# A hybrid attention and convolution layer: chain blocks placed behind scores, output projection before token sums, a first up-projection by column part

## The chip, the cores and the metric

The kernel runs on one core of a Trainium2 chip. The metric is the time of one execution on the device in microseconds (us), as the median of several. A core has a matrix engine (TensorE, PE in the profile, with PEld for its weight loads), a vector engine (VectorE, DVE), a scalar engine (ScalarE, ACT), a general engine (GpSimd, POOL) and an engine that only issues transfers (SyncE, SP); each works through its own instructions in order and waits for the others by semaphores.

## The reference

One layer of a diffusion backbone works on 1024 latent tokens and 256 context tokens of width 1024, all in float32:

```python
h = _rmsnorm(x, norm1_g) * (1.0 + sc1) + sh1
proj = h @ w_in
a = attend(q, k, v)                      # 8 heads of 64
hyo = _hyena(hy, k_f, filt_bias)         # 512 channels, two long convolutions by FFT
merged = concat([_rmsnorm(a, g_a), _rmsnorm(hyo, g_h)])
x = x + g1 * (merged @ w_out)
h2 = _rmsnorm(x, norm2_g) * (1.0 + sc2) + sh2
u = _dwconv3(h2 @ w_up, ffn_conv_w, ffn_conv_b)
gate, up = jnp.split(u, 2, axis=-1)
x = x + g2 * ((jax.nn.silu(gate) * up) @ w_down)
```

Context tokens attend among themselves; a latent token attends to a window of 8 by 16 latent tokens with a learned bias by relative position, and to 256 cached context keys, in one softmax. The norm of the attention group is taken over its 512 channels for each token. After the layer stands a last norm.

## The kernel before, in words

The kernel is written against a planner: the program traces instructions in some order, that order is their priority, and the planner simulates the engines and gives each of them, whenever it falls free in the simulation, the ready instruction of the highest priority. `tc.high_priority(offset=n)` lets a block count as if it had been traced n instructions earlier (later, if n is negative). `tc.issue_after(ins)` sets what the block traces on the engine of `ins` behind `ins` in that engine's order. Memory is given out by pools on two stacks, a left and a right one; with `reuse_waits="tile"` a new tile waits only for the old tiles whose bytes it takes.

Precise products are made of three fast ones: operands are split in a high part (ACT) and a low part (DVE or POOL), and `mm3` (lines 116 to 118) multiplies high by high, high by low and low by high.

The stages around the change, in order of time:

- **Input projection and chains.** The long convolutions are five chains (`chain(j)`, four blocks of 128 latent channels and one for the context), each of eight phases: for each of two convolutions a forward transform on PE (line 805, with `dftf`) with twiddles on ACT and DVE (817 to 819), sums and the product with the filter spectrum on DVE (826 to 847, the spectrum K loaded by SP at 840), the sums back with twiddles (852 to 864), and a backward transform on PE (877) with gating on DVE (882 to 890). Two lanes run them: chains 0, 2, 4 and chains 1, 3. `phases(n)` traces the next n phases in a fixed order of lanes (`turn2`). Sixteen are traced with a lead of 2000 instructions in the stage of the projection, the sixteenth being the first phase of chain 2. The rest is traced between the parts of the attention. The early ones have three PSUM banks for the transforms (`cA`), the later ones a single bank.
- **Attention** (`attend(p_)`, four pairs of heads). For each half b of a pair: score products on PE (`smm`, line 1068), bias and maximum on DVE (1089), exponentials on ACT (1102, 1103), then transposes of the weights on PE (1112), their copies to `pt` on ACT and DVE (1020, 1022), weighted values (1030), the reciprocal of the sums by way of PE (1040, 1045), and the result into `at4` (1159; context 1139). A pair's bias tables `tb` come by 48 small transfers that POOL issues (967), and wait for the last reader of the pair before. The context attention is traced last in pairs 0 to 2 and first in pair 3. A pair yields three times: after the scores of b = 0, after its values, and after the scores of b = 1.
- **Weights of the output projection.** Eight blocks of rows, k = 0 to 7, are loaded by SP (1205) and split by `wo_split` (ACT 1197, DVE 1198). Rows of k below 4 meet attention channels, the others convolution channels. The pool stands on the right stack, on the bytes of the chains. The raw rows `wor` have two buffers by turns, so the load of block k waits for the split of block k - 2; block 7 goes in two halves through a smaller one.
- **Token sums** (`token_scales`). The squares of the attention output, summed over channels for each token, give its scale `rsa` and the inverse `ria` by which the convolution half is brought to the same scale. `asq` holds the squares of pairs 0 to 2 summed, `sq` those of pair 3. For each block of 128 tokens PE multiplies a column of ones by the tile (line 1227), both tiles into the same sum; then DVE, POOL (a power, 1231), DVE, PE (a reversal of order, 1234) and DVE.
- **Output projection**, ten blocks of 128 tokens in the order 8, 9, 0, 4, 1, 2, 3, 5, 6, 7 (8 and 9 are the context). `att_split` (1291, 1292) splits a block of `at4` into `ar`; `omm(n, 0)` makes its half of the product with k = 0 to 3. `hyena_split` loads the convolution output y (1304), scales it (which needs `ria`), transposes it (1312) and splits it into `mr`; `omm(n, 1)` adds that half. Each half is 24 matmuls of 512 columns; three blocks can be under way (six banks). `post` adds the residue (it needs `rsa` and the gate rows g1), norms the row (1357, 1358), transposes it (1366) and writes it to hA (blocks 8, 9, 0, 4) or hB (the others).
- **Up-projection.** A Strassen-like scheme with seven products for each of 22 column blocks f, in the order 0, 1, 4, 5, 2, 6, 3. The left factors are sums `S` of quarters of the weight, split into `ws` tiles (121, 122); the right ones are sums of quarters of hA (256 columns, part s = 0) and of hB (384 columns, part s = 1), split into `Ta[p]` and `Tb[p]` (1263, 1264). `Ta[0..2]` and `Tb[0..1]` are split inside the loop of the output projection, the others behind it. `up(f, ...)` runs product after product, each for both parts; `cp` copies a sum out of its bank into `pc` (part 0) and a piece of `acc` (part 1). The tiles of pool `ffn` (`S`, `pc`, every third `ws`) take the bytes of hA and hB; those of pool `wsx` hold the gate rows g1 first.

Of the kernel before, what the change touches and what calls it, by code (L numbers as in the profile page):

```python
# [11 lines left out]
F32 = mybir.dt.float32  # L12
# [7 lines left out]
P = 128  # L20
D = 1024
# [65 lines left out]
def _build(nc, tc, top, V, A, G, T, Q, I, O, dbg, upto):  # L87
# [677 lines left out]
    with tc.high_priority(offset=2000):  # L765
        Q.dma_start(out=dftf.rearrange("p a b -> p (a b)"), in_=I["t_dft"].flatten().rearrange("(p x) -> p x", p=P))
        Q.dma_start(out=idft.rearrange("p a b c -> p (a b c)"), in_=I["t_idft"].flatten().rearrange("(p x) -> p x", p=P))

    S4B, TB = 3, 1
    CHP = 2000  # L770

    def chain(j):
# [22 lines left out]
        for o in range(2):  # L795
# [3 lines left out]
            for h in range(2):  # L799
                hs = slice(h * P, (h + 1) * P)  # L800
                for rp in range(2):
                    pa = bk("cA")
                    xs = slice(rp * 256, (rp + 1) * 256)
                    for i in range(2):
                        T.matmul(pa[:, i * 256:(i + 1) * 256], dftf[:, i, hs], uv[:, i, xs], start=True, stop=True)
                    pv = pa.rearrange("p (i r c) -> p i r c", i=2, r=2)
                    if not lat:
                        A.copy(Gv[:, h, :, 2 * rp:2 * rp + 2], pv)
                        continue
                    for ri in range(2):  # L810
                        r = 2 * rp + ri
                        if r == 0:
                            A.copy(Gv[:, h, :, 0], pv[:, :, 0])
                            continue
                        c, s, ns = tw_chain(h, r)
                        t = cp.tile([P, 2, P], F32, tag=f"t{b_}", name="t", bufs=TB)
                        A.activation(t[:, 0], pv[:, 1, ri], AF.Copy, scale=ns)
                        A.activation(t[:, 1], pv[:, 0, ri], AF.Copy, scale=s)
                        V.scalar_tensor_tensor(Gv[:, h, :, r], pv[:, :, ri], c, t, op0=ALU.mult, op1=ALU.add)
# [88 lines left out]
                next(lanes[turn2.pop(0)], None)  # L908

    with tc.high_priority(offset=CHP):  # L910
        phases(16)
    cbk.close()
    cbk = Banks("bkd", "right", "tile", cA=(1, 1))
    for _ in ada:
# [137 lines left out]
    def attend(p_):  # L1052
# [12 lines left out]

        def smm(outs, qc, kc):
            for h in range(2):
                T.matmul(outs[h], q[hs[h], qc], kc(hs[h]), start=True, stop=True, tile_position=(DH * h, 0),
                         skip_group_check=True)

        def scores(cb, l, l2, j):

# [71 lines left out]
        for b in range(2):  # L1144
            l, l2 = stat("l", 8), stat("l2", 8)
            for j in range(2):
                scores(2 * b + j, l, l2, j)
            yield
            V.tensor_add(l, l, l2)
            av = bk("av")  # L1150
            for j in range(2):
                cb = 2 * b + j
                for kt in range(2):
                    ps = turn(lambda h, i: Pc[cb][:, h, i, kt * P:(kt + 1) * P])
                    av_mm(av, 256 * j, vs[:, 10 + kt], ps, kt == 0)
                for vt, ps in local(cb):
                    av_mm(av, 256 * j, vt, ps, False)
            bs = recips(l, 8)
            V.tensor_mul(dst[:, 2 * b:2 * b + 2], av.rearrange("p (b r c) -> p b r c", b=2, r=16),
                         bs.rearrange("p (b r c) -> p b r c", b=2, r=16))  # L1160
            if b == 0:
                yield
# [6 lines left out]

    for p_ in range(4):  # L1170
        for n, _ in enumerate(attend(p_)):
            phases(2 - n % 2)
        phases(2)
    ces.close()
    cbk.close()
# [15 lines left out]
    sh2 = wo_.tile([P, 2, KC], F32, name="sh2")  # L1191
    V.tensor_copy(sh2.rearrange("p s (c j) -> p s c j", j=2), mods[:, 3].rearrange("p j (c s) -> p s c j", s=2))
    wo = []

    def wo_split(hi, lo, k, cs, w):
        g = grg[:, k:k + 1]
# [3 lines left out]
    for k in range(KC):  # L1200

        parts = [(slice(0, D), ("wh7", "wl7")[k % 2])] if k < 7 else [(slice(c, c + 512), "ot") for c in (0, 512)]
        for cs, tag in parts:
            w = wo_.tile([P, cs.stop - cs.start], F32, tag=tag, name="wor", bufs=1)
            Q.dma_start(out=w, in_=wsrc[:, k, cs])
            if cs.start == 0:
                hi, lo = [wfirst[i // 3][:, i % 3] for i in (2 * k, 2 * k + 1)] if k < 3 else \
                    [wo_.tile([P, D], F32R, tag=f"w{x}{k}", name=f"w{x}{k}", bufs=1) for x in "hl"]
            wo_split(hi, lo, k, cs, w)
        wo.append((hi, lo))  # L1210

    def tokens(t, i):
# [4 lines left out]

    def token_scales():

        sq = tp.tile([P, LT], F32, tag="q1", name="sq", bufs=1)  # L1220
        for cs in (slice(LL, LT), slice(0, LL)):
            A.activation(sq[:, cs], at4[:, 3, cs], AF.Square)
        ps = bk("X")
        for a, b in ((8, 10), (0, 8)):
            for i in range(a, b):
                for t in (asq, sq):
                    T.matmul(ps[:, 2 * i:2 * i + 2], tokens(t, i), ones2, start=t is asq, stop=t is sq,
                             skip_group_check=True)
            m, r = ria[:, a:b], rsa[:, a:b]
            V.tensor_scalar(m, ps[:, 2 * a:2 * b:2], 1.0 / 512, EPS, op0=ALU.mult, op1=ALU.add)  # L1230
            G.tensor_tensor(r, m, mhalf.to_broadcast([P, b - a]), op=ALU.pow)
            V.tensor_mul(m, m, r)
            pr = bk("X")
            T.matmul(pr[:, 0:b - a], jrev, m, start=True, stop=True)
            u = 4 if a == 0 else 1
            V.tensor_copy(m[:, u:], pr[:, u:b - a])

    token_scales()
    es.close()
    abk.close()  # L1240

# [155 lines left out]
    def second_sums(t):  # L1397
        cs = slice(t * P, (t + 1) * P)
        if t == 0:
            ts = acp.tile([P, 3, 4, NS[1]], F32, tag="acc", name="tsb", bufs=1)  # L1400
            b.update({4: ts[:, 0], 5: ts[:, 1], 3: ts[:, 2]})
        V.tensor_sub(b[4][..., cs], b12[..., cs], b11[..., cs])
        V.tensor_sub(b[5][..., cs], b22[..., cs], b[4][..., cs])
# [60 lines left out]

    def wstile():
        ring["ws"] += 1
        if ring["ws"] % 3:
            return wsx.tile([P, 2, 512], F32R, tag="ws", name="ws", bufs=2)
        return fpl.tile([P, 2, 512], F32R, tag="ws", name="ws", bufs=1)

# [34 lines left out]
    def blocks(f):  # L1505
# [5 lines left out]
        for p in PORD:  # L1511
            if p in (0, 1, 3):
                src = {0: a11, 1: a12, 3: a22}[p]
            else:
                src = fpl.tile([P, 512], F32, tag="S", name="S", bufs=2)
                s[p] = src
                if p == 4:
                    V.tensor_add(src, a21, a22)
# [10 lines left out]
    def up(f, rg, ru):  # L1529

        ws = blocks(f)

        def prod(outs, p, start, stop):
            w = next(ws)
            for s in range(2):
                t = TT[s][p]
                for k in range(4):
                    ks = slice(k * P, (k + 1) * P)
                    mm3(outs[s][:, :NS[s]], w[:, 0, ks], w[:, 1, ks], t[:, 0, k], t[:, 1, k], start and k == 0,
                        stop and k == 3)  # L1540

        def cp(src):
            t = [fpl.tile([P, NS[0]], F32, tag="pc", name="pc", bufs=2), pcb[ring["pc"] % 2]]
# [10 lines left out]
            return [bk(tag) for _ in range(2)]  # L1554

        a = two("a")
        prod(a, 0, True, True)
        p1 = cp(a)
        b = two("b")
        prod(b, 1, True, True)  # L1560
        add(rg, 0, p1, b)
        c = two("c")
        prod(c, 4, True, True)
# [19 lines left out]
    for f in range(NFF):  # L1583
# [8 lines left out]
        t = fpl.tile([P, 2, 2, 256], F32, tag="wt", name="wt", bufs=1)  # L1592
        for r in range(2):
            Q.dma_start(out=t[:, r], in_=wdn[i, :, r, :, cs])
        up(f, rg, ru)
        V.tensor_sub(t[:, 0, 0], t[:, 0, 1], t[:, 0, 0])
        V.tensor_sub(t[:, 0, 1], t[:, 1, 1], t[:, 0, 1])
        V.tensor_sub(t[:, 1, 1], t[:, 1, 1], t[:, 0, 0])
# [233 lines left out]
```

## Time and profile before

| | |
|---|---|
| times of three runs | 1839.21, 1842.02, 1844.18 us; median 1842.02 |
| profiled execution | 1843.86 us, of which the span of the instructions is 1841.9 us |
| busy in the span | PE 1725.3 us (94%), DVE 1367.1 (74%), ACT 893.9 (49%), POOL 396.7 (22%) |
| mean granted clock of TensorE | 0.964 |
| chain of waits that ended last | PE 38%, DVE 14%, DMA 8%, issue 4%, ACT 3%, POOL 1% |

A line of the timeline gives the start, the duration, the engine, the source line, the operation, what it writes and reads, shapes and count, and in brackets how long the engine stood before it and for whom. Matmuls are pipelined and overlap in such lines, so the distance of two starts says more than a duration. A float32 matmul of the program stands as two instructions.

### The profile page before, as it was taken

The page shows a single profiled execution, that of the slowest core. Times are in us where ns is not written, and L with a number is a line of the kernel's source. Part 1 is how long each engine was busy: PE and PEld are TensorE (multiplying, and loading weights), DVE is VectorE, ACT ScalarE, POOL GpSimd, SP SyncE. Part 2 cuts the span into 40 slices and gives each one's busy share as a digit, 9 for nine tenths or more (in the row PEclk, how much of TensorE's full clock was granted, in tenths as well). Part 3 has the DMA queues.
Part 4 walks back from the last instruction along what each step waited for, and adds up shares of the span by engine and source line. Part 5 has one row for each costly group of instructions (what it writes and reads, how often), then busy time and mean ns, then how long its engine had stood idle before and what let it go on. Part 6 is the DMA issues. An engine that isn't in the chain of part 4 may idle for free.

```text
span 1841.9 us, 27359 instructions
## 1 busy us (share of the span) xinstructions
PE 1725.3 (94%) x9999; PEld 1453.2 (79%) x9999; DVE 1367.1 (74%) x2166; ACT 893.9 (49%) x1852; POOL 396.7 (22%) x487
## 2 busy tenths in 40 slices
PE   5899999999996898898997999999999999999997
PEld 1588788788884455566886999999999999888786
DVE  4658957853778798973558798889777877566797
ACT  4645535533334566664556444444444444443452
POOL 2266565674117442600110000000000000000001
PEclk7899999999997799998998999999999999999999
DMA  7424354356546332516231554454222123934653
GB/s 247 157 87 135 105 176 131 112 132 192 168 143 194 96 106 69 147 35 213 78 109 50 165 167 151 157 164 163 82 65 73 60 65 102 350 112 142 207 185 132
DMA packets 202440, 249.78 MB, mean 136 GB/s; under 512 B 21923, under 2 KB 147988, under 8 KB 202050
## 3 DMA queue, kind: packets, MB, share of 16 engines
q1 hardware_dynamic: 190360, 230.75, 38.8%
q0 software_dynamic: 10240, 16.46, 3.7%
q8 instruction: 79, 1.29, 0.3%
q10 hardware_dynamic: 1705, 0.82, 0.2%
q14 instruction: 56, 0.45, 0.1%
HBM read 176.75 MB, written 71.20 MB: 135 GB/s over the span
## 4 chain that ended last, share of the span: by engine, by line
PE 38%; DVE 14%; DMA 8%; issue 4%; ACT 3%; POOL 1%; DVEq 0%; POOLq 0%; ACTq 0%; SPq 0%
PE psd L116 6%; PE psd L117 6%; PE psd L118 6%; PE psa L116 3%; PE psa L117 3%; PE psa L118 3%; DMA wt<-in_w_down_dram 2%; PE psc L118 2%; PE psc L117 2%; PE psc L116 2%; PE psb L117 2%; PE psb L118 2%; PE psb L116 2%; DMA tdr<-wt 2%; POOL tb L967 1%
## 5 line engine op out<-in xcount | busy, mean ns | idle before, releaser
L116 PE MATMUL psp<-hh,wh 128*128 128x512 f32 (+1 forms) x552 | 200.6, 363 | 1.9 <-ACT wh L121 1.9
L118 PE MATMUL psp<-hh,wl 128*128 128x512 f32 (+1 forms) x552 | 199.5, 362 | 1.0 <-POOL wl L122 1.0
L117 PE MATMUL psp<-hl,wh 128*128 128x512 f32 (+1 forms) x552 | 198.9, 360 | 0.0
L1747 POOL TENSOR_TENSOR rs<-rs,mhalf 128x1 f32<-128x1 f32 x10 | 7.7, 776 | 816.0 <-DVE rs L1746 816.0
L116 PE MATMUL psa<-T,ws 128*128 128x256 f32 (+1 forms) x528 | 166.0, 314 | 3.9 <-ACT rows L1546 2.7
L117 PE MATMUL psa<-T,ws 128*128 128x256 f32 (+1 forms) x528 | 165.3, 313 | 0.0
L118 PE MATMUL psa<-T,ws 128*128 128x256 f32 (+1 forms) x528 | 164.7, 312 | 0.0
L116 PE MATMUL psd<-wd,gs 128*128 128x512 f32 x360 | 140.8, 392 | 3.1 <-ACT gs L121 3.1
L117 PE MATMUL psd<-wd,gs 128*128 128x512 f32 x360 | 141.0, 392 | 0.0
L118 PE MATMUL psd<-wd,gs 128*128 128x512 f32 x360 | 123.3, 390 | 1.7 <-DVE gs L122 1.6
L116 PEld LDWEIGHTS psp<-hh,wh 128*128 128x128 f32 x552 | 104.9, 190 | 23.2 <-issue 7.4
L118 PEld LDWEIGHTS psp<-hh,wl 128*128 128x128 f32 x552 | 104.9, 190 | 16.4 <-POOL wl L122 1.2
L117 PEld LDWEIGHTS psp<-hl,wh 128*128 128x128 f32 x552 | 104.8, 190 | 14.1 <-issue 0.4
L116 PE MATMUL psc<-T,ws 128*128 128x384 f32 (+1 forms) x352 | 110.1, 313 | 5.8 <-ACT ws L121 5.8
L118 PE MATMUL psc<-T,ws 128*128 128x384 f32 (+1 forms) x352 | 110.0, 313 | 0.3 <-DVE ws L122 0.3
L967 POOL DMA_DIRECT2D tb<-rpw x192 | 100.5, 531 | 45.1 <-DVE m L1089 31.7
L117 PE MATMUL psc<-T,ws 128*128 128x384 f32 (+1 forms) x352 | 110.1, 313 | 0.0
L117 PE MATMUL psb<-T,ws 128*128 128x384 f32 (+1 forms) x352 | 109.4, 311 | 0.0
L118 PE MATMUL psb<-T,ws 128*128 128x384 f32 (+1 forms) x352 | 109.4, 311 | 0.0
L116 PE MATMUL psb<-T,ws 128*128 128x384 f32 (+1 forms) x352 | 109.2, 310 | 0.0
L116 PEld LDWEIGHTS psa<-T,ws 128*128 128x128 f32 x528 | 101.4, 192 | 5.7 <-ACT rows L1546 4.0
L117 PEld LDWEIGHTS psa<-T,ws 128*128 128x128 f32 x528 | 101.3, 192 | 0.0
(405 smaller groups left out, 4785.8 us busy)
## 6 DMA issues: line engine op xcount, KB each, us to landing
wada<-in_w_ada_dram SPq DMA_DIRECT2D x48, 512.0 KB
wr<-in_w_up_dram SPq DMA_DIRECT2D x44, 512.0 KB
gr<-gdr SPq DMA_DIRECT2D x44, 320.0 KB
wr<-in_w_in_dram SPq DMA_DIRECT2D x23, 512.0 KB
wt<-in_w_down_dram SPq DMA_DIRECT2D x44, 256.0 KB
tdr<-wt SPq DMA_DIRECT2D x44, 256.0 KB
gdr<-cv SPq DMA_DIRECT2D x22, 512.0 KB
wr<-tdr SPq DMA_DIRECT2D x20, 512.0 KB
```

The costliest lines, as they stand in the source:

```text
L116: T.matmul(out, ah, bh, start=start, stop=False, skip_group_check=True)
L117: T.matmul(out, ah, bl, start=False, stop=False, skip_group_check=True)
L118: T.matmul(out, al, bh, start=False, stop=stop, skip_group_check=True)
L967: blast[0] = G.dma_start(out=tv[:, :, a * 8:a * 8 + 64], in_=rpw[var, :, 2 * p_:2 * p_ + 2, :, d * 8:d * 8 + 64].rearrange("q h u x -> q ( ...
L1747: G.tensor_tensor(rs, rs, mhalf, op=ALU.pow)
```

## The change

It has four parts.

1. Sixteen phases traced early become fifteen. Between the parts of a pair three phases are traced where there were two, and two where there was one. While the attention runs, the forward transforms of a chain's first convolution are set on PE behind the last score product traced (`gate`, `smm.last`).
2. `wo_split` for k above 3, and `token_scales`, count as traced 150 instructions later. `sq` moves from tag q1 to tag q0; the two tiles of squares are added on DVE first, and PE sums one tile instead of two.
3. For f = 0 the first two products are run part by part: product 0 and 1 for the columns of hA, then product 0 and 1 for those of hB. `up(0)` counts as traced 120 instructions earlier.
4. The third `ws` tile is taken from pool `wsx`, and the sum `S` of product 4 for f = 0 from unused bytes of `acc`.

```diff
+    gate = []
...
-                    for i in range(2):
-                        T.matmul(pa[:, i * 256:(i + 1) * 256], dftf[:, i, hs], uv[:, i, xs], start=True, stop=True)
+                    with tc.issue_after(gate[0]) if gate and o == 0 else ExitStack():
+                        for i in range(2):
+                            T.matmul(pa[:, i * 256:(i + 1) * 256], dftf[:, i, hs], uv[:, i, xs], start=True, stop=True)
...
-        phases(16)
+        phases(15)
...
             for j in range(2):
                 scores(2 * b + j, l, l2, j)
+            gate[:] = [smm.last]
             yield
...
         for n, _ in enumerate(attend(p_)):
-            phases(2 - n % 2)
+            phases(3 - n % 2)
         phases(2)
...
+    WLATE = 150
...
-            wo_split(hi, lo, k, cs, w)
+            with tc.high_priority(offset=-WLATE if k > 3 else 0):
+                wo_split(hi, lo, k, cs, w)
...
-        sq = tp.tile([P, LT], F32, tag="q1", name="sq", bufs=1)
-        for cs in (slice(LL, LT), slice(0, LL)):
+        sq = tp.tile([P, LT], F32, tag="q0", name="sq", bufs=1)
+        ps = bk("X")
+        for cs, a, b in ((slice(LL, LT), 8, 10), (slice(0, LL), 0, 8)):
             A.activation(sq[:, cs], at4[:, 3, cs], AF.Square)
-        ps = bk("X")
-        for a, b in ((8, 10), (0, 8)):
+            V.tensor_add(sq[:, cs], sq[:, cs], asq[:, cs])
             for i in range(a, b):
-                for t in (asq, sq):
-                    T.matmul(ps[:, 2 * i:2 * i + 2], tokens(t, i), ones2, start=t is asq, stop=t is sq,
-                             skip_group_check=True)
+                T.matmul(ps[:, 2 * i:2 * i + 2], tokens(sq, i), ones2, start=True, stop=True, skip_group_check=True)
...
-    token_scales()
+    with tc.high_priority(offset=-WLATE):
+        token_scales()
...
-            ts = acp.tile([P, 3, 4, NS[1]], F32, tag="acc", name="tsb", bufs=1)
+            acc = acp.tile([P, 5 * D], F32, tag="acc", name="tsb", bufs=1)
+            ts = acc[:, 0:12 * NS[1]].rearrange("p (a k c) -> p a k c", a=3, k=4)
+            b["S"] = acc[:, 12 * NS[1]:]
...
-        if ring["ws"] % 3:
+        if ring["ws"] % 3 or ring["ws"] == 3:
...
-                src = fpl.tile([P, 512], F32, tag="S", name="S", bufs=2)
+                src = fpl.tile([P, 512], F32, tag="S", name="S", bufs=2) if f or p != 4 else b["S"]
...
+        if f == 0:
+
+            b = two("b")
+            w0 = prod(a, 0, True, True, (0,))
+            w1 = prod(b, 1, True, True, (0,))
+            prod(a, 0, True, True, (1,), w0)
+            p1 = cp(a)
+            prod(b, 1, True, True, (1,), w1)
...
-        up(f, rg, ru)
+        with tc.high_priority(offset=0 if f else 120):
+            up(f, rg, ru)
```

More of the change, by code (lines that the diff above doesn't have):

```diff
@@ L1067, in smm @@
             for h in range(2):
-                T.matmul(outs[h], q[hs[h], qc], kc(hs[h]), start=True, stop=True, tile_position=(DH * h, 0),
-                         skip_group_check=True)
+                smm.last = T.matmul(outs[h], q[hs[h], qc], kc(hs[h]), start=True, stop=True,
+                                    tile_position=(DH * h, 0), skip_group_check=True).ins
         def scores(cb, l, l2, j):
@@ L1218, in token_scales @@
     def token_scales():
-        sq = tp.tile([P, LT], F32, tag="q1", name="sq", bufs=1)
-        for cs in (slice(LL, LT), slice(0, LL)):
+        sq = tp.tile([P, LT], F32, tag="q0", name="sq", bufs=1)
+        ps = bk("X")
+        for cs, a, b in ((slice(LL, LT), 8, 10), (slice(0, LL), 0, 8)):
             A.activation(sq[:, cs], at4[:, 3, cs], AF.Square)
-        ps = bk("X")
-        for a, b in ((8, 10), (0, 8)):
+            V.tensor_add(sq[:, cs], sq[:, cs], asq[:, cs])
             for i in range(a, b):
-                for t in (asq, sq):
-                    T.matmul(ps[:, 2 * i:2 * i + 2], tokens(t, i), ones2, start=t is asq, stop=t is sq,
-                             skip_group_check=True)
+                T.matmul(ps[:, 2 * i:2 * i + 2], tokens(sq, i), ones2, start=True, stop=True, skip_group_check=True)
             m, r = ria[:, a:b], rsa[:, a:b]
@@ L1531, in up, with prod @@
         ws = blocks(f)
-        def prod(outs, p, start, stop):
-            w = next(ws)
-            for s in range(2):
+        def prod(outs, p, start, stop, parts=(0, 1), w=None):
+            w = w or next(ws)
+            for s in parts:
                 t = TT[s][p]
@@ L1540, in prod @@
                         stop and k == 3)
+            return w
         def cp(src):
@@ L1556, in up @@
         a = two("a")
[L1557 to L1560, printed above, removed]
+        if f == 0:
[5 more added lines that the diff above has]
+            prod(b, 1, True, True, (1,), w1)
+        else:
+            prod(a, 0, True, True)
+            p1 = cp(a)
+            b = two("b")
+            prod(b, 1, True, True)
         add(rg, 0, p1, b)
```

## The prediction

> **What bounds the kernel now.** I read the busy times first (TensorE 94% of the span, so only places where it idles or runs at a low clock can pay), then the busy time by stretch of the three places that the change touches, then each engine's timeline at the seams. In the stretches the columns are: length, busy time of PE, weight load, DVE, ACT, POOL, then granted clock, DMA share, GB/s.
>
> ```profile
> 576.00:600.00 24.00, 11.83 (x40) 8.40 (x40) 21.57 (x39) 10.58 (x38) 17.05 (x32) 0.71 0.82 242
> 600.00:640.00 40.00, 31.78 (x152) 16.79 (x150) 30.76 (x70) 23.20 (x80) 18.51 (x37) 0.78 0.37 96
> 640.00:780.00 140.00, 125.36 (x777) 76.62 (x775) 127.48 (x266) 92.26 (x296) 63.02 (x118) 0.96 0.39 107
> 780.00:842.00 62.00, 60.65 (x382) 37.24 (x378) 42.16 (x95) 39.81 (x113) 0.00 (x0) 1.00 0.21 71
> 842.00:862.00 20.00, 12.86 (x63) 11.40 (x64) 10.26 (x16) 9.06 (x12) 2.38 (x2) 0.69 0.43 129
> 862.00:987.00 125.00, 125.00 (x584) 101.52 (x582) 70.22 (x116) 65.54 (x114) 11.99 (x19) 0.98 0.33 117
> 987.00:1022.00 35.00, 19.42 (x97) 18.03 (x96) 29.38 (x40) 19.55 (x28) 1.29 (x10) 0.71 0.18 58
> ```
>
> The attention stage (576 to 842, with the convolution chains mixed in) starts bound by VectorE (DVE 21.57 of 24) and ends bound by TensorE (60.65 of 62). The output projection (862 to 987) is TensorE without a gap, so whatever time its start gains passes through to its end. The seams at 842 and 987 are where TensorE idles and its clock falls to about 0.7.
>
> **Part A: the chains in the attention stage.** A program line asks for a phase of a chain after each yield of a pair of heads. A pair yields three times, so it drove 2+1+2 phases and 2 behind it, 7; now 3+2+3 and 2, 10. The 25 phases left (15 instead of 16 are placed early) then end in the middle of pair 2, instead of the 24 ending in pair 3. Also, the first transform of a new chain is now issued on PE behind the last score product traced before it.
>
> The rows of the chain alone (instructions that touch its tiles; same columns without POOL):
>
> ```profile
> 576.00:842.00 266.00, 59.46 (x209) 40.84 (x208) 140.32 (x207) 28.76 (x76) 0.92 0.39 109
> 780.00:842.00 62.00, 15.81 (x62) 10.95 (x62) 18.46 (x29) 4.46 (x10) 1.00 0.21 71
> ```
>
> DVE in the whole stage is 21.57+30.76+127.48+42.16 = 222.0 us, 140.3 of it chain, so 81.7 attention, 20.4 a pair. PE is 11.83+31.78+125.36+60.65 = 229.6, 59.5 of it chain, so 42.5 a pair for attention. Attention is PE work, a chain is DVE work. Today the last pair's stretch still holds 18.5 of DVE and 15.8 of PE for the chain, and PE is full there.
>
> After: all of the chain and about 2.5 pairs lie in a front that DVE bounds, 140.3 + 2.5 x 20.4 = 191.3 us of DVE; behind it 1.5 pairs of pure attention that PE bounds, 1.5 x 42.5 = 63.8, at today's use of 60.65/62 = 0.98 some 65. The end then hangs on how well DVE is used in the front. At 1.00 it ends at 576+191.3+65.1 = 832; at 0.94 at 845; at 0.88, which is today's use from 576 to 780 ((21.57+30.76+127.48)/204), at 858. Today it is 846. I take 0.94, between today's mean and the 1.0 bound: DVE idles today mostly from 600 to 640 (9.2 us), where the change puts chain work that the gate has held back. What the gate frees:
>
> ```profile
> 583.07 5.50 PE L805 MATMUL pscA<-s,dftf 128*128 128x256 f32 x16 [6.61 <-DMA s<-lxd]
> 588.49 1.20 PE L1068 MATMUL psS<-k,q 64*128 64x264 f32 x8
> 594.31 3.75 PE L877 MATMUL pscA<-s,idft 128*128 128x256 f32 x8 [4.61 <-DVE s L819]
> ```
>
> ```profile
> 598.07 0.42 DVE L1089 CUSTOM_DVE_ANT_0 Pl<-psS,tb 128x264 f32<-128x264 f32 x1
> ```
>
> Chain 2's first block waits 6.61 us for its load with the first scores queued behind it on PE; with the gate the scores can go when that wait begins, at 576.5. But their first DVE step comes only at 598.07, since DVE is full of chain work from 576 to 600; so the 11 us earlier scores are worth only the DVE work of chain 2 that no longer stands in front of them. That gain is inside the use of 0.94, not added to it. Held behind the gate are only the chain's own matmuls (16 each time); its loads on SP aren't held, its ACT and DVE steps follow. Its transforms use one PSUM bank instead of three, now for chain 2 as well. **A: 846.4 to 844.6, -2; bounds -14 and +12** (use 1.00 and 0.88).
>
> **Part B: the seam into the output projection.** PE, then ACT, DVE and SP:
>
> ```profile
> 845.78 0.65 PE L1030 MATMUL psav<-pt,vs 128*64 128x256 f32 x4
> 846.37 0.38 PE L1227 MATMUL psX<-ones,asq 128*128 128x2 f32 x2
> ...
> 855.52 0.60 PE L1227 MATMUL psX<-ones,sq 128*128 128x2 f32 x2
> 859.63 0.56 PE L1234 MATMUL psX<-ria,jrev 128*128 128x8 f32 x2 [3.50 <-DVE ria L1232]
> 861.32 0.79 PE L116 MATMUL psd<-w,ar 128*128 128x512 f32 x1 [1.12 <-ACT ar L1291]
> ...
> 881.47 0.40 PE L116 MATMUL psd<-wh,mr 128*128 128x512 f32 x1
> ```
>
> ```profile
> 860.04 0.72 ACT L1197 ACTIVATE wh<-wor,vec 128x512 fp32r<-128x512 f32 x1 [3.35 <-DMA wor<-in_w_out_dram]
> 860.66 1.12 ACT L1291 CAST ar<-at 128x512 fp32r<-128x512 f32 x2
> 870.87 0.63 ACT L1306 ACTIVATE jk<-y 128x512 bf16<-128x512 f32 x1 [9.09 <-DMA y<-hyd]
> ```
>
> ```profile
> 844.52 1.28 DVE L1198 SCALAR_TENSOR_TENSOR wl<-wor,vec,wh 128x1024 fp32r<-128x1024 f32 x1 [0.77 <-ACT wh L1197]
> ```
>
> ```profile
> 828.32 0.37 SPq L898 DMA_DIRECT2D hyd<-s  x1
> 831.17 26.66 SPq L1205 DMA_DIRECT2D wor<-in_w_out_dram  x9
> ```
>
> From the last attention product (846.4) to the first projection product (861.32) PE does token sums, waits for POOL's power in between, and the projection's operand `ar` is queued on ACT behind the last weight split, which waited for its load. None of that is needed: the attention half of a token uses weights 0 to 3, whose last split (844.52) is done by 845.8, and the first two tokens are context, long finished. The old `sq` lay in q1, whose bytes `ar` takes next (worked out from the tile sizes in order of allocation); in q0 it no longer blocks it. What still blocks `ar` is the last use of the transposed tiles `pt` (845.78). So `ar` at about 847 and PE at about 848: 13.3 us earlier. The token sums don't vanish: L1227 takes 9.75 us for 40 instructions (846.37 to 856.1); with the tiles added first there are 20, 4.9 us, now between projection products. 13.3 - 4.9 = 8.4. The two added DVE sums (128x256 and 128x1024) cost about as much as the split above, 1.6 together; they lie under PE. The weights come earlier as well: their loads begin when the last chain store (828.32) frees that memory, and the chains end before that; their splits move under the last pair, where ACT has 39.81 and DVE 42.16 of 62.
>
> What is late next is the hyena half. Three tokens' attention halves take 861.32 to 881.47, 20 us, then `mr` must be there. It needs y (loaded behind the wor loads, landed 870.87) and the token sums. From 848 PE runs dry at 868. The y loads no longer stand behind 26.66 us of weight loads; they need only the memory of the P tiles, so they can land before 860. But the sums are now 150 places later, about behind the third token's products; from them to `mr` lies a chain of DVE, POOL, PE, ACT, PE, ACT, DVE, some 6 us by what the same chain takes here (3.50 of it is the wait in the row). If they run that late PE idles up to 5 us. The new place of `sq` also delays the second g1 row buffer, and what is behind it on SP, until the sums are read; g1 is needed first by the third token. **B: -8; bounds -13** (no wait, and the sums hidden in gaps of PE) **and -4** (8.4 less 5).
>
> The Trainium skill ("TensorE: Matmul & The Clock Gate", Part 1: The HAM clock gate) says that the clock drops to half after an idle window of about 3.4 us and comes back after as long a busy one. The rows agree in kind: 0.69 in the seam, 0.98 behind it. By that rule a seam without such a gap would keep the full clock and the sums would cost half, 2.4 us less; by the rows alone nothing is known of a shorter gap.
>
> **Part C: the seam into the up-projection.** PE; DVE; ACT:
>
> ```profile
> 997.10 1.97 PE L1366 MATMUL pst<-ident,xr 128*128 128x128 f32 x8 [8.22 <-ACT xr L1358]
> 998.72 0.56 PE L116 MATMUL psa<-T,ws 128*128 128x256 f32 x1
> ...
> 1007.69 0.33 PE L118 MATMUL psb<-T,ws 128*128 128x384 f32 x1
> 1013.77 0.58 PE L116 MATMUL psc<-T,ws 128*128 128x256 f32 x1 [5.75 <-ACT ws L121]
> ```
>
> ```profile
> 976.02 1.76 DVE L1264 TENSOR_TENSOR T<-hB,T 128x1536 fp32r<-128x1536 f32 x1 [0.59 <-ACT T L1263]
> ...
> 1003.44 1.75 DVE L1264 TENSOR_TENSOR T<-tsb,T 128x1536 fp32r<-128x1536 f32 x1
> ...
> 1010.72 1.74 DVE L1264 TENSOR_TENSOR T<-tsb,T 128x1536 fp32r<-128x1536 f32 x1
> 1012.39 0.68 DVE L1518 TENSOR_TENSOR S<-wr 128x512 f32<-128x512 f32 x1
> ```
>
> ```profile
> 1010.89 0.37 ACT L1546 COPY pc<-psa 128x256 f32<-128x256 f32 x1 [3.29 <-DVE T L1264]
> ```
>
> PE stands 8.22 us for the last token's transposes, with products 0 and 1 (998.72 to 1008.0) behind them, though these read operands whose last split is the one at 976.02. Moved 120 places ahead and taken column part by column part, they fit into that gap. Then product 4: its sum S lay in memory of hB, free only when the last operand is split (1012.39); in `acc` and with a slot of the other `ws` pool it comes earlier, and the product can run from about 1005, as its operand is split (1003.44), instead of 1013.77. Behind it product 5 waits as before: its own S and the copy `pc` still lie in hB's bytes (1010.89), and DVE, 29.38 busy of 35, has the same splits to do. So what is gained is about one product: 1013.77 less 1007.69 is 6.1, less the rest of that wait. **C: -4; bounds -6 (that whole gap) and 0** (DVE's last split decides everything).
>
> **Sum.** -2 - 8 - 4 = -14. The profiled execution took 1843.86 (span 1841.9), so 1830 for it; the median of three is 1842.02, 1.84 lower, and the forecast is **1828**.
>
> **Rivals.**
> 1. *DVE packs the front fully and the seams close*: A -14, B -13, C -6, so -33: 1809. For it: DVE has room from 600 to 640, 30.76 of 40. Against: DVE waits for ACT in most chain steps. 0.15.
> 2. *The seams open again one step later*: the hyena half waits for the sums (B -4), product 5 for the last splits (C 0), A -2; -6: 1836. It is also what comes out if the planner puts the sums where they were and only their halving counts. For it: the 9.09 us wait for y and the 1010.89 row. 0.22.
> 3. *Slower: VectorE as the bound of the first pairs.* Ten phases a pair put all of the chain in front of 1.5 pairs in which DVE then has little to do. If it is used at 0.84 there, the front takes 191.3/0.84 = 228, the stage ends at 576+228+65 = 869, +22; with B and C kept (-12) +10: 1852. It decides from a use of 0.88 downwards (191.3/0.88 = 217, +12, as much as B and C bring). Today's 0.88 stands just at that point, which speaks for it; that TensorE, not DVE, holds parts of today's front (31.78 of 40 with DVE at 30.76) speaks against. 0.13.
>
> The forecast itself has 0.45; the last 0.05 is a mixture near no change (today's 0.88 with B and C: 1842). A measurement of this kernel can tell 0.3%, 5.5 us, from no change. Faster by more: the forecast, the first rival and half of the second, 0.71; slower 0.13; the rest 0.16. The range reaches from beyond the first rival's near side, 1806, to 1844, and leaves the third rival out.
>
> **What would show it.** A: chain stores end near 780 instead of 828; PE without chain lines in the last pair, DVE over 0.92 from 576 to there; the first scores near 577. B: the first psd product within 3 us of the last psav, half as many L1227, the first product with `mr` 20 us later without a gap. C: psa and psb before the last L1366, psc near 1005 after its own start shifted by A and B. I am wrong if the last psav is later than 846 by more than a few us (A), if PE stands before `mr` (B), or if product 5 starts no earlier after the last L1366 than now (C).

## The result and the profile after

The changed kernel takes 1875.3 us (median of 4) where the kernel before took 1843.1 beside it: a ratio of 1.0167, 95% interval 1.0146 to 1.0188. It is 32 us slower. The forecast was 14 us faster, and its range (1806 to 1844) does not hold the time. The profiled execution took 1872.14 us, its span is 1870.4 (before 1841.9).

Five of the stretches of the changed kernel, in the columns used before the prediction:

```profile
576.00:600.00 24.00, 6.29 (x25) 3.21 (x22) 16.49 (x34) 8.79 (x34) 17.64 (x33) 0.57 0.81 242
600.00:640.00 40.00, 33.39 (x177) 18.47 (x177) 21.47 (x54) 21.19 (x73) 22.64 (x44) 0.91 0.25 48
640.00:780.00 140.00, 122.84 (x772) 75.15 (x770) 121.91 (x264) 90.69 (x297) 55.99 (x104) 0.98 0.34 93
780.00:842.00 62.00, 51.22 (x284) 33.55 (x286) 47.91 (x100) 35.15 (x108) 0.00 (x0) 0.92 0.22 69
862.00:987.00 125.00, 113.62 (x515) 91.82 (x515) 68.50 (x116) 65.25 (x108) 13.37 (x19) 0.93 0.44 148
```

VectorE was to be fuller in the front of the attention. It is emptier: 16.49 + 21.47 + 121.91 = 159.9 us of the 204 from 576 to 780, against 179.8 before. TensorE's timeline shows where that begins, and the two seams after it:

```profile
575.47 1.87 PE L1070 MATMUL psS<-k,q 64*128 64x264 f32 x8
592.63 2.08 PE L1070 MATMUL psS<-k,q 64*128 64x256 f32 x8 [15.29 <-DVE m L1091]
...
610.25 1.13 PE L1070 MATMUL psS<-k,q 64*128 64x256 f32 x8
611.31 1.13 PE L807 MATMUL pscA<-s,dftf 128*128 128x256 f32 x4
...
855.60 0.65 PE L1032 MATMUL psav<-pt,vs 128*64 128x256 f32 x4
...
860.22 1.97 PE L879 MATMUL pscA<-s,idft 128*128 128x256 f32 x8 [2.02 <-DVE s L891]
867.37 3.89 PE L1231 MATMUL psX<-ones,sq 128*128 128x2 f32 x16 [5.19 <-DVE ria L1233]
876.26 0.57 PE L1237 MATMUL psX<-ria,jrev 128*128 128x8 f32 x2 [4.57 <-DVE ria L1235]
878.21 0.79 PE L116 MATMUL psd<-w,ar 128*128 128x512 f32 x1 [1.38 <-ACT ar L1295]
...
1016.58 1.97 PE L1370 MATMUL pst<-ident,xr 128*128 128x128 f32 x8 [7.38 <-ACT xr L1362]
1018.20 0.56 PE L116 MATMUL psa<-T,ws 128*128 128x256 f32 x1
1027.63 0.39 PE L116 MATMUL psc<-T,ws 128*128 128x256 f32 x1 [1.03 <-ACT ws L121]
```

The first scores come 13 us earlier, about as forecast (575.47, before 588.49). But the scores behind them wait 15.29 us for VectorE, and chain 2's first transform, which the wait (`gate`) sets behind the last score of the first half pair, starts at 611.31 instead of 583.07, 28 us late. The attention's last product is late too (855.60, before 845.78), and the last chain's backward transform stands behind it (860.22). From the last score steps to the next work VectorE has a gap, since it has nothing of chain 2 to do:

```profile
596.63 0.28 DVE L1101 SCALAR_TENSOR_TENSOR m<-m,n 128x2 f32<-128x2 f32 x2
605.76 0.69 DVE L1022 COPY pt<-psX 128x512 f32<-128x512 f32 x1 [8.85 <-PE psX L1114]
```

SP's timeline shows how the delay spreads and what it ends in:

```profile
641.74 6.84 SPq L842 DMA_DIRECT2D K<-Kd  x2
648.95 0.80 SPq L792 DMA_DIRECT2D s<-lxd  x2
651.32 0.95 SPq L897 DMA_DIRECT2D hyd<-s  x2
...
864.17 0.37 SPq L900 DMA_DIRECT2D hyd<-s  x1
867.03 7.73 SPq L1209 DMA_DIRECT2D wor<-in_w_out_dram  x5
```

Chain 1's store (651.32, before 612.24) and chain 3's load (648.95, before 610.47) belong to the other lane and are late too, by 39 us. Their place in SP's order, behind the spectra K (the K load of 641.74 stood 59.7 us for VectorE), is not what held them to the end: each goes within 0.1 us of the end of a gating step of chain 1 on VectorE (L892 ends at 651.29, L891 at 648.89). VectorE's last step ahead of chain 1's backward transform, and then chain 2's last first-convolution transform and that backward transform on TensorE, show why these steps are late:

```profile
593.64 0.48 DVE L866 SCALAR_TENSOR_TENSOR s<-s,tw,t 128x256 f32<-128x256 f32 x1 [0.76 <-ACT t L865]
```

```profile
626.39 1.13 PE L807 MATMUL pscA<-s,dftf 128*128 128x256 f32 x4 [0.78 <-DVE s L821]
...
634.58 1.99 PE L879 MATMUL pscA<-s,idft 128*128 128x256 f32 x8
```

Chain 1's data are ready at 594.1, but its backward transform starts at 634.58 (before: 594.31), behind all four transforms of the held chain 2. The two chains share the one PSUM bank of the later phases, and chain 2's first phase is traced ahead of chain 1's last. That the shared bank is what ties them is read from the program and from this order; no run has a second bank.

The last chain store comes at 864.17 instead of 828.32, and 2.9 us later come the first weights of the output projection, whose memory the chains hold (before: 831.17). ACT then has no split to make until they land, and `ar` stands behind two such waits:

```profile
870.60 2.35 ACT L1201 ACTIVATE w<-wor,vec 128x1024 fp32r<-128x1024 f32 x2 [7.97 <-DMA wor<-in_w_out_dram]
876.50 1.15 ACT L1201 ACTIVATE w<-wor,vec 128x1024 fp32r<-128x1024 f32 x1 [3.55 <-DMA wor<-in_w_out_dram]
877.56 1.12 ACT L1295 CAST ar<-at 128x512 fp32r<-128x512 f32 x2
```

So the first projection product starts at 878.21 instead of 861.32, +17. Product 4 of the up-projection is at +14 (1027.63 against 1013.77), the end of the span at +28.5: another 14.6 us are lost behind product 4, in stages that no term of the forecast dealt with.

### The profile page after: what moved, and what is told of

Same layout as the page of the kernel before. It is cut to its first block, busy times and chain, and to the rows that moved or that the text cites. A ratio compares the mean times of both kernels' runs of the same rounds, so it can differ in the third digit from the quotient of the medians.

```text
span 1870.4 us, 27223 instructions
## 1 busy us (share of the span) xinstructions
PE 1720.8 (92%) x9979; PEld 1448.3 (77%) x9979; DVE 1359.5 (73%) x2168; ACT 889.9 (48%) x1852; POOL 396.3 (21%) x487
## 4 chain that ended last, share of the span: by engine, by line
PE 56%; DVE 19%; DMA 11%; ACT 6%; issue 4%; POOL 2%; SPq 1%; ACTq 0%; DVEq 0%; POOLq 0%
PE psd L118 5%; PE psd L116 5%; PE psd L117 5%; PE psp L116 4%; PE psp L118 4%; PE psp L117 4%; PE psa L116 3%; PE psa L117 3%; PE psa L118 2%; DMA wt<-in_w_down_dram 2%; PE psb L117 2%; PE psb L116 2%; PE psb L118 2%; PE psc L118 2%; PE psc L116 2%
## 5 line engine op out<-in xcount | busy, mean ns | idle before, releaser
L116 PE MATMUL psa<-T,ws 128*128 128x256 f32 (+1 forms) x528 | 163.6, 313 | 4.1 <-ACT pc L1553 4.0
L117 PE MATMUL psa<-T,ws 128*128 128x256 f32 (+1 forms) x528 | 164.3, 311 | 0.0
L118 PE MATMUL psa<-T,ws 128*128 128x256 f32 (+1 forms) x528 | 159.4, 311 | 1.2 <-DVE ws L122 1.2
L116 PEld LDWEIGHTS psp<-hh,wh 128*128 128x128 f32 x552 | 104.8, 190 | 23.2 <-issue 7.4
L118 PE MATMUL psc<-T,ws 128*128 128x384 f32 (+1 forms) x352 | 107.3, 315 | 6.5 <-DVE ws L122 6.5
L116 PE MATMUL psc<-T,ws 128*128 128x256 f32 (+1 forms) x352 | 108.9, 313 | 1.0 <-ACT ws L121 1.0
L117 PE MATMUL psc<-T,ws 128*128 128x256 f32 (+1 forms) x352 | 109.8, 312 | 0.0
L116 PE MATMUL psb<-T,ws 128*128 128x256 f32 (+1 forms) x352 | 107.7, 311 | 1.1 <-ACT ws L121 1.1
L117 PE MATMUL psb<-T,ws 128*128 128x256 f32 (+1 forms) x352 | 108.6, 310 | 0.0
L118 PE MATMUL psb<-T,ws 128*128 128x256 f32 (+1 forms) x352 | 103.2, 310 | 0.0
```

The costliest lines, as they stand in the source:

```text
L116: T.matmul(out, ah, bh, start=start, stop=False, skip_group_check=True)
L117: T.matmul(out, ah, bl, start=False, stop=False, skip_group_check=True)
L118: T.matmul(out, al, bh, start=False, stop=stop, skip_group_check=True)
```

## The experiments

The theory from these rows was: the wait costs, by way of a serial lane of chains and the weights. Rivals: ten phases a pair crowd VectorE; the missing sixteenth early phase; the new places of parts B and C. Runs e1 to e4 share the runs of the kernel before that they are compared with, and so do e5 to e8 and e9 to e11; e12 has its own.

**e1: no wait.** The changed kernel with

```diff
-with tc.issue_after(gate[0]) if gate and o == 0 else ExitStack():
+with ExitStack():
```

> The changed kernel without the wait: the first transform of a new chain is issued when its data are there. Fifteen early phases and ten a pair stay, and so do parts B and C. Gate theory (the wait holds chain 2's first block back by 28 us, 583 to 611, each lane of chains is a serial line of some 15.5 us a phase, and the weights of the output projection wait for the last chain's memory): the last chain store comes back from 864 to within 6 us of 830, the first weight load from 867 to about 833, and the time falls by 25 to 40, to 1835 to 1850. Rival, ten phases a pair crowd VectorE: the last store stays behind 855 and the time above 1865. Rival, the sixteenth early phase is what is missing: the store comes near 843 and the time near 1855.

1855.32 us, 20.0 below the changed kernel; last chain store at 830.60, first weight load at 833.46. Store and load are back where the theory had them, so it is the wait that delays the chains. But the time falls by 20 and not by the 25 to 40 expected, and it stays 1.0064 (1.0045 to 1.0083) times that of before: something else costs as well. The rival of the sixteenth phase gave this time, but with the store near 843.

**e2: phases as before, wait kept.**

```diff
-phases(15) ... phases(3 - n % 2)
+phases(16) ... phases(2 - n % 2)
```

> The changed kernel with the phases placed as before (sixteen early, seven a pair), the wait kept on every block that is placed after the first scores. Chain 2's first block is then placed early, ahead of any score, so the wait holds only the blocks of chains 3 and 4. Gate theory: chain 2 starts near 583 again and its lane is not held there; chain 3's first block (616.96 before) is held by little; last store within 8 us of 828 and time 1835 to 1850. Rival, ten phases a pair crowd VectorE: the same time, but then the run without the wait must stay slow. Rival, the planner's new places for B and C cost: 1860 or more.

1855.82 us (1.0065, 1.0047 to 1.0082). Time and last store (839.18) miss what was expected. The profiled execution is the slowest of the ten (1862.63) and starts its chains 4 us late (587.10, before 583.07). With chain 2's first block placed early, the wait on chains 3 and 4 costs nothing that the time shows: e4, which has none, takes 1856.19. It does lengthen the lane by some 7 us (the table below). So the 20 us of the wait come from chain 2's first block.

**e3: part A alone**, B and C undone (wrappers `high_priority(offset=0)` around `up` and around `wo_split` stayed).

> The kernel before with part A alone (wait, fifteen early phases, ten a pair); parts B and C are undone. If part A alone delays the chains: last store near 864 as in the changed kernel, first weight load near 867, and, as the old seam needs 30 us from there to the first projection product, this product at about 897; time 1872 to 1885. If B or C is what costs: within 8 us of 1843.

1876.77 us (1.0180, 1.0155 to 1.0206); last store 862.75, weights 865.60. But the first projection product stands at 879.24, not at 897: the 30 us between weights and product of before were not needed, as 13.6 are enough here.

**e4: B and C alone**, no wait, old phases.

> The kernel before with parts B and C, without the wait and with the phases of before. By the forecast's terms B -8 and C -4: 1829 to 1834. By what the changed kernel shows (19 of the 36 us made good at the first projection product, 5 more at product 4, some 14 lost again behind it): first projection product 842 to 850 instead of 861, time 1830 to 1845. If the places of B and C cost by themselves: over 1846.

1856.19 us (1.0072, 1.0048 to 1.0095): the two parts that were to bring 12 cost 13. e1 against e4 (1855.32, 1856.19) is the phase rate by itself, ten a pair or seven, fifteen early or sixteen. The medians differ by 1 us; as the two intervals are 7 and 9 us wide, a cost of a few us isn't excluded, but one of 20 is, and the rival of a crowded VectorE falls. And e3, without B and C, loses the same behind product 4 as all the others. What they share is the wrapper, which the change puts around the up-projection of every block, with offset 0 for all but the first.

**e5: the wrapper with offset 0 alone**, on the kernel before.

```diff
-        up(f, rg, ru)
+        with tc.high_priority(offset=0):
+            up(f, rg, ru)
```

> The kernel before with one thing added: the call of the up-projection of every block stands inside a high_priority(offset=0), as it does in the changed kernel for all blocks but the first. Nothing else is changed, and nothing is computed otherwise. All five traces of changed kernels so far, the one with part A alone among them (which kept this wrapper), take 842.0 to 846.3 from product 4's first matmul to the end, where the kernel before takes 828.1; before the chip the order of 383 of 2168 VectorE instructions differs. Theory: offset zero is not nothing to the planner, and this wrapper costs 14 to 18: time 1855 to 1862. Rival: it is nothing, and what is lost behind product 4 comes from the later or other arrival of the stage; then within 4 of 1843.

1853.60 us, 1.0058 (1.0043 to 1.0072), so +10.7, somewhat less than expected. The longest of TensorE's waits behind the last transposes, of the kernel before (first) and of e5:

```profile
PE psc L116 <- ACT ws L121: 5.8, 1, 5.8
PE psd L116 <- ACT gs L121: 3.1, 1, 3.1
PE psa L116 <- ACT rows L1546: 2.7, 6, 0.9
PE psd L118 <- DVE gs L122: 1.6, 1, 1.6
```

```profile
PE psc L116 <- ACT ws L121: 6.5, 1, 6.5
PE psa L116 <- ACT pc L1546: 6.1, 3, 2.4
PE psd L118 <- DVE gs L122: 5.6, 2, 4.0
PE psc L118 <- DVE ws L122: 1.6, 3, 0.8
```

The columns are the whole wait in us, how often, and the longest. The order of work on DVE, ACT and SP is another from the second block on: what is traced behind a wrapped block (the sums of the down weights, the short convolution) is mixed otherwise with the splits of the next. TensorE waits for copies (`pc` 6.1) and splits that used to be in time; all its waits there sum to 23.2 us, before 14.7. The down-projection, from its first product to the end of the span, takes 281.9 us in e5 and 281.9 to 285.2 in e1 to e4 and the changed kernel, but 274.3 to 276.1 in the kernel before and in the runs from e6 on.

Why a wrapper with offset 0 does this can be read from the planner's count (the number that stands for an instruction's place in the order of tracing) while the program is traced: at its end, `high_priority` sets the count back to where it stood ahead of the block. One call of `up` is 204 counts long. In the kernel before, its calls begin at 7176, 7401 and 7626, 225 apart; in e5 at 7176, 7197 and 7218, 21 apart. So what is traced behind a wrapped block, and all later blocks, rank as if that block had never been traced. If the count is put forward again behind each wrapper, the program comes out with the order of the kernel before on TensorE, VectorE, ScalarE and SyncE, without a difference. That was read from built programs and not run.

**e6: B and C without that wrapper** (only the first block keeps its offset of 120).

```diff
-with tc.high_priority(offset=0 if f else 120):
+with ExitStack() if f else tc.high_priority(offset=120):
```

> Parts B and C as in e4, with the high_priority wrapper only around the first block's up-projection (offset 120) and none around the others. Theory of the zero offset: 14 to 18 faster than e4, 1836 to 1843, that is 0 to 8 below the kernel before, as B and C are worth 2.3 (last attention product to first projection product 13.2 in e4, 15.5 before) and 5.6 (last projection product to product 4 21.2 against 26.8). Rival: equal to e4, 1856.

1842.48 us (0.9995, 0.9982 to 1.0007): 13.7 below e4, as expected (around one block, the wrapper sets the count back only once). B and C together are worth nothing that shows.

**e7: part B alone.**

> The kernel before with part B alone. The order on TensorE still has all token sums ahead of the first projection product, so only their halving counts: 1 to 5 below the kernel before. By the forecast's own term -8 (bounds -13, -4).

1842.17 us (0.9991, 0.9979 to 1.0002). From the last attention product to the first projection product it is 12.4 us, before 15.5. On e4, where the seam is the same, TensorE and ACT show why it is not 1.5:

```profile
847.94 3.90 PE L1231 MATMUL psX<-ones,sq 128*128 128x2 f32 x16 [2.00 <-DVE sq L1229]
855.70 0.57 PE L1237 MATMUL psX<-ria,jrev 128*128 128x8 f32 x2 [3.86 <-DVE ria L1235]
856.12 0.77 PE L116 MATMUL psd<-w,ar 128*128 128x512 f32 x1
```

```profile
851.08 1.15 ACT L1201 ACTIVATE wh<-wor,vec 128x1024 fp32r<-128x1024 f32 x1 [3.38 <-DMA wor<-in_w_out_dram]
853.58 0.72 ACT L1201 ACTIVATE wh<-wor,vec 128x512 fp32r<-128x512 f32 x1 [1.35 <-DVE wl L1202]
854.20 1.12 ACT L1295 CAST ar<-at 128x512 fp32r<-128x512 f32 x2
```

All sums still stand ahead of the projection, and `ar` still stands behind weight splits that wait for their loads. The offset of 150 moved neither: with 0, 400 or 1000 in its place, e4's program has the same order on TensorE, VectorE, ScalarE and SyncE (read from built programs, not run).

**e8: part C alone**, the wrapper around the first block only.

> The kernel before with part C alone, the wrapper around the first block only. The order on TensorE still has products 0 and 1 behind the last token's transposes, so only the new memory of product 4's operands counts: by e4's seam 5.6 less, 3 to 7 below the kernel before if nothing is given back in the up-projection. By the forecast's own term -4 (bounds -6, 0). If the offset of 120 for one block also disturbs what follows: 0 or slower.

1836.87 us (0.9967, 0.9955 to 0.9978), 6 below the kernel before: the best of all here, and in the expected band. Products 0 and 1 did not move into the gap: in all these kernels they stand behind the last transposes (998.56 here, before 998.72). Product 4 starts at 1008.00 instead of 1013.77, but only its first matmuls do, as TensorE and DVE show:

```profile
1008.00 0.38 PE L116 MATMUL psc<-T,ws 128*128 128x256 f32 x1 [0.74 <-ACT ws L121]
...
1012.97 0.58 PE L118 MATMUL psc<-T,ws 128*128 128x256 f32 x1 [4.11 <-DVE ws L122]
```

```profile
1010.55 1.75 DVE L1269 TENSOR_TENSOR T<-tsb,T 128x1536 fp32r<-128x1536 f32 x1
1012.22 0.69 DVE L122 TENSOR_TENSOR ws<-tsb,ws 128x512 fp32r<-128x512 f32 x1
```

The low half of its weight tile is split on DVE behind the last operand, in the order of the program, though its memory no longer asks for it.

**e9: all parts, no wrapper around later blocks** (e6's edit on the changed kernel).

> The changed kernel with all three parts, but the high_priority wrapper only around the first block's up-projection. If the costs add (wait 20, zero offset 11 to 14, parts B and C -1): 11 to 14 below the changed kernel, 1860 to 1865, and 17 to 22 above the kernel before, all of it from the wait. If the zero offset's cost hangs on the arrival of the stage: anywhere from 1850 to 1875.

1861.82 us (1.0105, 1.0088 to 1.0123), in the expected band: 13.5 below the changed kernel, and 19.3 above e6, the same without wait and phases (measured against other runs of the kernel before, 1844.04 and 1843.68). The costs add.

**e10: as e9, the wait on the first score product.**

```diff
-            gate[:] = [smm.last]
+                if not gate and h == 1:
+                    gate[:] = [m_]
```

The new lines stand in `smm`; `m_` is the matmul just traced.

> As e9, but every new chain waits only for the first score product of the first pair, not for the last one traced; the first scores still go ahead of chain 2's first block. Theory (the harm is the 28 us for which the wait holds chain 2's first block, and it passes through a serial lane to the last chain store and the weights): chain 2's first block starts within 8 us of the first score, 576 to 585, the last store comes near 826 to 836, the first weight load 3 later, time 1838 to 1847. Rival (scores ahead of the chain cost by themselves, as VectorE gets score work when the chain needs it): last store behind 845, time over 1850.

1843.01 us (0.9996, 0.9984 to 1.0008), 18.8 below e9. The scores still go first, and the chain follows at once:

```profile
575.09 2.10 PE L1070 MATMUL psS<-k,q 64*128 64x264 f32 x8
581.85 2.08 PE L807 MATMUL pscA<-s,dftf 128*128 128x256 f32 x4 [4.66 <-DMA s<-lxd]
592.25 2.08 PE L1070 MATMUL psS<-k,q 64*128 64x256 f32 x8 [8.33 <-DVE m L1093]
594.26 2.07 PE L807 MATMUL pscA<-s,dftf 128*128 128x256 f32 x4
```

Last store 833.44, weights 836.31. Scores first do no harm, and bring nothing: the next scores wait for VectorE.

**e11: e8 with e10's wait and part A's phases.**

> Part C alone as in e8, with the wait on the first score product and the phases of part A (fifteen early, ten a pair). If scores ahead of the chain are worth the 10 us by which they come earlier, faster than e8's 1836.9 by up to 8; if, as the theory has it, the chains' latency and VectorE set the stage, the same as e8 within 4.

1849.97 us (1.0035, 1.0022 to 1.0047): neither expectation; 13 above e8. At product 4 it is 1 us behind e8 (1009.01, 1008.00), at the first down product 6.9 (1569.87, 1562.97). Its source from the output projection on is e8's, but the order that the planner finds is not: a few dozen of some 1050 instructions that DVE has from the first `ws` split on stand elsewhere. In the up-projection, TensorE waits 6.0 us for the copies of line 1555 (e8 3.3) and 2.1 for splits that e8 has in time, which is most of the 5.9 us that this stage is longer. The built programs tell more: in the up-projection and behind it, e11 has on TensorE, VectorE and ScalarE exactly the order of e6, and e10 that of e8. From product 4 to the first down product the first pair takes 560.2 (e6) and 560.9 us, the second 555.0 (e8) and 551.2. So what this stage takes goes with the order that the planner finds; which of its differences costs was not tried. The lane of chains is longer as well (251.1 us, e8 245.5). That these two make up all of the 13 is not shown.

**e12: only the memory of part C** (`S` of product 4 in `acc`, the third `ws` tile from `wsx`).

> Of part C only the memory: the sum S of product 4 lies in the accumulator tile and the third weight tile of the first block in the other pool. Products 0 and 1 stay in their old order and no offset is used. If the memory is what part C is worth: within 2 of e8's 1836.9 and product 4 at least 4 nearer to the last projection product than before (26.8). If the order by column part and the offset of 120 carry it: within 2 of the kernel before, 1843 to 1844.

1840.66 us (0.9986, 0.9974 to 0.9999), between the two: it starts product 4 at 21.2 behind the last projection product, as e6 (before 26.8), and is worth some 2.6. The rest of e8's 6 seems to come with the order by column part and the offset, though the two intervals overlap.

**A lane has nearly one length.** From chain 2's first transform to the last chain store, 16 phases of one lane, in us:

| kernel | first transform | last store | length |
|---|---|---|---|
| before | 583.07 | 828.32 | 245.2 |
| changed | 611.31 | 864.17 | 252.9 |
| e1, no wait, ten a pair | 578.87 | 830.60 | 251.7 |
| e2, wait on chains 3 and 4, seven a pair | 587.10 | 839.18 | 252.1 |
| e4, no wait, seven a pair | 580.23 | 825.44 | 245.2 |
| e9, wait | 610.32 | 863.50 | 253.2 |
| e10, wait on the first score | 581.85 | 833.44 | 251.6 |

Seven phases a pair without a wait give 245.2; ten a pair, or a wait, give 251.6 to 253.2. Tracing the phases closer did not shorten a lane, and the chains end when they began plus some 250. The 6.5 us by which e1's lane is longer than e4's may come from the bank: with fifteen early phases, chain 2's first four transforms share one PSUM bank instead of three and take 13.3 us in e1, where they took 5.5 before. No run has the one without the other.

**The sum.** Wait 20.0 (changed less e1; e9 less e10 gives 18.8), wrapper 13.5 (changed less e9; e4 less e6 gives 13.7), phases -0.9 (e1 less e4), B and C -1.2 (e6 less before): 31.4 of the 32.2 measured. The changed kernel, e1, e4, e6 and the kernel before follow each other edit by edit, so terms taken along them must come near the whole; what carries the sum is that wait and wrapper were each measured twice. The phases and B and C can't be told from nothing.

## Why the prediction was wrong

**Part A, -2 forecast, some +19 measured: the step that failed** is the first, "The 25 phases left (15 instead of 16 are placed early) then end in the middle of pair 2". It took the place where a phase is traced for the place where it ends. A lane is a line of steps on PE, ACT, DVE and SP that wait for each other, some 250 us long. Tracing its phases closer did not shorten it (e1 against e4), and holding its first block moves its end. The last attention product came at 855.60 instead of 845.78, the sign of being wrong that the forecast had named for A. The forecast said "Held behind the gate are only the chain's own matmuls", and priced the hold at nothing, since it counted DVE's work and not the lane's length. The "only" was wrong too: chain 1's backward transform stood behind them (634.58 instead of 594.31). And "its loads on SP aren't held" was true of chain 2's first loads (581.56), not of the next spectrum (641.74 instead of 602.88). The one PSUM bank, which the forecast names without a price, costs chain 2's first transforms 7.8 us in e1.

The use of 0.94 rested on "DVE idles today mostly from 600 to 640 (9.2 us)". The rows shown there have 12.5 us of DVE's idle time from 640 to 780, and 9.2 of 24.2 is not most of it. The third rival had the sign, and the poor use of VectorE that it asked for (0.84 or less; 0.78 measured), but not the reason: ten phases a pair don't do it (e1 against e4), the wait does.

**Part B, -8 forecast, -1.5 measured (not to be told from nothing).** With "the chains end before that" false, the weights came 36 us later, not earlier. That alone is not it: e7 has the weights on time and gains 3.1 at the seam. The step "`ar` at about 847" failed, since `ar` stays behind the splits of rows 4 to 7 on ACT (854.20 in e4), which the offset was thought to move. The memory was judged rightly: in the kernel before, the program has `ar` wait for the last token sum, in e4 for no product behind the last of the attention. The halving was right: 20 instructions for the sums instead of 40, at the old price (3.90 for 16 on e4, 9.75 for 40 before). The rival "if the planner puts the sums where they were and only their halving counts" is what happened.

**Part C, -4 forecast, -6 measured alone (e8), nothing beside B (e6).** "they fit into that gap" failed: the products stayed behind the transposes. That product 4 comes earlier was right, and that "DVE's last split decides", its bound of 0, was right for the third matmul. The forecast took it that what a seam gains stays gained. That hangs on the order that the planner then finds for the up-projection. From product 4 to the first down product it takes 552.1 us in the kernel before, 553.0 in e7, and with the two orders named at e11 555.0 and 551.2 (e8, e10) or 560.2 and 560.9 (e6, e11). So e6 gains 3.0 us at the seam of B and 5.6 at that of C, and gives 8.1 back behind product 4. No term of the forecast was about this order.

**The term that was missing, +13.5:** the wrapper around the later blocks. The forecast read `offset=0 if f else 120` as a change to the first block, and offset 0 as nothing. But a wrapper also sets the count back at its end. On the kernel before, without any of the rest, it costs 10.7 (e5).

## What to carry to other kernels

Before a serial chain of small steps is held back, measure its length from first to last step in the trace: it ends when it starts plus that length, however densely its steps are traced, and the next stage's memory may hang on its end. Hold such a chain behind the first instruction that must precede it, not the last (e10 against e9, 18.8 us). A scheduling wrapper with an offset of zero is an edit, since it sets the count back for all that is traced behind it; read its effect from the order of the instructions there, and where a priority is to move something, see that the order has moved before counting the gain, and that it has not moved in the stages behind (e6 against e10).

## What the runs showed of the hardware

The clock does not follow the busy time that the profile records. Stretches of the old seam in the kernel before, then of the same seam in e4 (the granted clock is the third number from the end):

```profile
845.70:850.00 4.30, 3.57 (x23) 2.96 (x21) 2.39 (x6) 3.42 (x4) 0.72 (x1) 0.94 0.43 155
850.00:856.10 6.10, 6.10 (x27) 6.04 (x26) 2.57 (x2) 1.69 (x3) 0.00 (x0) 0.50 0.28 86
```

```profile
844.10:847.90 3.80, 0.35 (x2) 0.30 (x2) 2.91 (x7) 2.92 (x3) 0.72 (x1) 0.83 0.42 139
847.90:851.90 4.00, 3.90 (x16) 3.81 (x16) 1.18 (x1) 0.82 (x1) 0.00 (x0) 0.50 0.33 122
...
856.10:860.00 3.90, 3.90 (x10) 3.13 (x11) 2.11 (x4) 0.72 (x1) 0.00 (x0) 0.50 1.00 254
860.00:866.00 6.00, 6.00 (x26) 4.79 (x26) 0.27 (x1) 1.12 (x1) 0.00 (x0) 0.98 0.98 373
```

The products of two columns that make the token sums keep TensorE busy for 6.10 of 6.10 us in the kernel before, and the clock stays at 0.50 all that time. Each of them loads its own 128x128 weights, and the weight load is as busy (6.04 of 6.10). In e4 the clock comes back only 3.9 us into the projection, whose first ten matmuls take as long as some seventeen at 0.98. The Trainium skill ("TensorE: Matmul & The Clock Gate", Part 1: The HAM clock gate) says that about 3.4 us of sustained matmuls bring the full clock; the projection agrees, the 6.10 us of token sums do not. So sums in a seam cost their own time and don't bring the clock back for what follows. Whether the projection would start at the full clock without them isn't shown, as in both kernels TensorE also waits behind them (3.50 and 3.86 us). The forecast's estimate that they cost half at the full clock has one row here, from e4: four of them took 0.61 us at 1.00 (0.15 each), against 0.24 each at 0.50, so six tenths and not half:

```profile
843.48 0.61 PE L1231 MATMUL psX<-ones,sq 128*128 128x2 f32 x4
```
